# A two-layer hybrid decoder trunk: compression products read the split token pairs, with three smaller moves between engines

## The chip, the cores and the metric

One core of a Trainium2 chip runs the whole program. The metric is device time in microseconds (us), lower is better. TensorE does the matrix products, VectorE and ScalarE the elementwise work, GpSimd some of the same, and all loads go through the queue of SyncE (SP). TensorE's clock has two levels, 1.2 and 2.4 GHz; the profile gives the granted clock as a share of the full one.

## The reference, cut to what matters

512 tokens, width 1024, two layers. Each layer projects the normed rows into the operands of three head groups, joins their outputs by one output projection, and adds a gated feed-forward (2816 wide) and a per-layer embedding. Three pieces matter here:

```python
def compress_blocks(kv, pos_emb, w1, w2):          # 31 blocks of 32 tokens, stride 16
    blocks = kv[:, idx] + pos_emb[:, None, :]
    blocks = blocks.transpose(0, 1, 3, 2, 4).reshape(b, n_cmp, g, NSA_CMP_LEN * d)
    return jax.nn.gelu(blocks @ w1) @ w2
...
    c = jnp.cumsum(log_f.astype(jnp.float32), axis=1).transpose(0, 2, 1)   # forgetting attention
    logits = q @ k * scale + c_blk[..., None] - c[:, :, None, :]
...
    hn = rms_norm(h, norm_ffn[i])
    h = h + (jax.nn.silu(hn @ w_ffn_gate[i]) * (hn @ w_ffn_up[i])) @ w_ffn_down[i]
```

The blocks are made once for keys and once for values, for two groups of heads, each of 64 features.

## The kernel before, in words

Every fp32 matrix product is made of three products of split operands: a high half in the reduced fp32 format that TensorE takes at full rate, a low half with the remainder, high times high, high times low and low times high (`mm3`, L221 to L225). So each operand costs a copy into the high half, on ScalarE, and a subtraction for the low half, on VectorE or GpSimd. Weights come in as raw tiles and are split in `halves` (L197 to L201), where GpSimd takes one subtraction in two or three (`lo_turn`).

A program places each instruction on its engine's queue in an order worked out from the order in the text, priorities (`prio`) and `issue_after`, which only says that one instruction stands behind another on the same engine. Each engine then works through its queue in order.

A layer's attention is a sequence of phases (`spec`, L1175). In each, one attention part is woven with projections as filler: `weave` takes from the stream that is behind by its share, and the numbers after `yield` are the shares in columns of products.

- The compression (`compress`, L563) is woven with the three projections of the stick-breaking heads. The key and value columns come first (`evac_c`, L553): for each of the four tiles of 128 tokens, the rows are rotated, doubled, transposed on TensorE, so that both halves of the partitions hold the same 64 features, and copied by two activations (L561). `blocks` (L567) adds the position embedding to the tokens, even tokens in the upper half of the partitions and odd ones in the lower, in four additions per pass on VectorE (L582), and splits the result into `bhl` by two copies and two subtractions (L589, L590). A pass is made for keys and one for values. `hidden` (L593) then runs 16 pairs of products for each: 128 columns with the high weights (L603), 64 with the low ones (L605), and the GELU chain on VectorE (L611 to L622). Its result is first needed when the selected-block heads begin.
- `forget_rows` (L825) takes the forget gates' logarithms, adds them up along the tokens in one scan on VectorE (L840), and lays the sums out in rows of two tiles that a product can read, with fills of ones and scalings, nearly all on VectorE (L838 to L851). It is called as part "FR" when the second selected-block group starts (L874 is the scores' maximum, L877 their exponential, L869 their products).
- The feed-forward's first unit starts with the first half of the tokens while the second half is still being normed: `part(..., slice(0, 256))` and then `slice(256, 512)` (L1241 to L1246). The norm (`rms_rows`, L328, and `normed`, L345) takes a power on GpSimd for each of the four token tiles (L335), scales the rows on VectorE in two halves (L368), transposes them on TensorE (L380), and splits them on ScalarE (L385) and VectorE (L388). `operand_sums` (L396) prepares sums of operand halves for later units that use seven products instead of eight; for the first half of the tokens it adds on GpSimd, for the second on VectorE (L406).

The small tiles of the GELU chain and the forget rows share four buffers ("e"), the larger ones fifteen ("u").

Of the kernel before, what the change touches and what calls it, by code (L numbers as in the profile page):

```python
# [19 lines left out]
P = 128  # L20
S = 512
# [21 lines left out]
def hybrid_trunk_kernel(  # L43
# [109 lines left out]
    ve.memset(mhalf, -0.5)  # L153

# [241 lines left out]
    def operand_sums(xact):  # L396
# [4 lines left out]
        for kh in range(2):  # L401
            F = utile([P, 2, 4, 256], F32, name="xF")
            for t in range(2):
                hi, lo = (xact.tiles[kh][j][:, :, t * 256:(t + 1) * 256] for j in range(2))
                whole[t, kh] = F[:, t]
                (ve if t else ge).tensor_tensor(F[:, t], f(hi), f(lo), op=ALU.add)  # L406
# [131 lines left out]
    def mixer(i):  # L538
# [10 lines left out]
        ckv = [utile([P, 2, 528], F32, name=f"ckv{j}") for j in range(2)]  # L549
        for t in ckv:  # L550
            ge.memset(t[:, :, S:], 0.0)

        def evac_c(tt, acc):  # L553
# [6 lines left out]
            for j in range(2):  # L560
                se.activation(ckv[j][:, :, tt * P:(tt + 1) * P], pt[:, 2 * j:2 * j + 2, :], AF.Copy)  # L561

        def compress():  # L563
# [3 lines left out]
            def blocks(which, pos, w1, w2):  # L567
# [8 lines left out]
                blk = utile([P, 16, 2, 32], F32, name="blk")  # L576
                tv = ckv[which].rearrange("p g (n l) -> p g n l", l=16)
                for hf in range(2):
                    for par in range(2):
                        r = slice(par * HD, (par + 1) * HD)  # L580
                        src = tv[r, :, hf:hf + 32, par::2].rearrange("p g n l -> p l g n")
                        ve.tensor_tensor(blk[r, 8 * hf:8 * hf + 8], src,  # L582
                                         peT[r, 8 * hf:8 * hf + 8][:, :, None, None].to_broadcast([HD, 8, 2, 32]),
                                         op=ALU.add)
                bhl = utile([P, 2, 16, 64], name="bhl")
                bf = blk.rearrange("p l g n -> p l (g n)")
                for hf in range(2):
                    r = slice(8 * hf, 8 * hf + 8)
                    se.activation(bhl[:, 0, r], bf[:, r], AF.Copy)  # L589
                    ve.tensor_tensor(bhl[:, 1, r], bf[:, r], f(bhl[:, 0, r]), op=ALU.subtract)  # L590
                state.append((w1, w2s, bhl))

            def hidden(which):  # L593
                w1, w2s, bhl = state[which]
# [14 lines left out]
                xx, yy, zz = x1[:, 0:64], x1[:, 64:128], x1[:, 128:192]  # L609
                se.activation(yy, acc[:, 64:128], AF.Copy)  # L610
                ve.tensor_tensor(xx, acc[:, 0:64], yy, op=ALU.add)  # L611
# [8 lines left out]
                gx = x1[:, 256:512].rearrange("p (g h n) -> p g h n", g=2, h=4)  # L620
# [39 lines left out]
            yield 500  # L660
# [164 lines left out]
        def forget_rows():  # L825
# [614 lines left out]
```

## Time and profile before

| | |
|---|---|
| median of 3 runs | 1554.16 us |
| lowest and highest run | 1549.36 and 1555.05 us |
| the profiled execution's own time | 1549.74 us |
| its span, first to last instruction | 1548.0 us |
| TensorE busy | 1490.1 us, 96% |
| VectorE (DVE) busy | 1004.0 us, 65% |
| ScalarE (ACT) busy | 809.3 us, 52% |
| GpSimd (POOL) busy | 650.3 us, 42% |
| granted TensorE clock, mean | 0.990 |

A row of the timeline gives start, length, engine, line, operation, the tiles written and read, their sizes, how many instructions were merged into the row, and in brackets how long the engine had been idle before and what ended that. PEld is the load of weights into TensorE, which overlaps its products. The lengths of successive products overlap; what one costs is read from the distance of their starts. A row of windows gives, for a stretch, the time in which each engine was busy, and the granted clock.

### The profile page before, as it was taken

What the parts mean: (1) busy time and instruction counts of PE and PEld (TensorE: products, weight loads), DVE (VectorE), ACT (ScalarE), POOL (GpSimd) and SP (SyncE); (2) the same over time, 40 slices, a digit from 0 to 9 for tenths busy, and PEclk for the clock granted to TensorE, in tenths of its full rate; (3) what the DMA queues carried; (4) which work ended last, traced back from release to release, by engine and by line L of the source; (5) the groups of instructions that cost most, each with busy time, mean ns of one, the idle gap of its engine ahead of it and who ended that gap; (6) DMA issues with size and microseconds to landing.
All of it is one profiled execution on the core that took longest, in us unless ns stands there. A gap on an engine that the chain in (4) does not pass through costs nothing.

```text
span 1548.0 us, 25774 instructions
## 1 busy us (share of the span) xinstructions
PE 1490.1 (96%) x9562; PEld 1313.8 (85%) x9562; DVE 1004.0 (65%) x1910; ACT 809.3 (52%) x1725; POOL 650.3 (42%) x666
## 2 busy tenths in 40 slices
PE   6999999998999999999999999999899999999998
PEld 5898887878999889988988888778799988998888
DVE  6777869768685257634386878786678833675253
ACT  5466676654544234433355767586545532454243
POOL 3323455554555234431233235465545542455323
PEclk9899999999999999999999999999999999999999
DMA  5421321131333323342224121211223233324321
GB/s 180 118 78 35 84 76 35 49 96 41 105 114 96 95 83 109 123 136 69 83 75 120 55 72 53 82 29 48 90 69 109 89 116 95 107 92 143 109 69 55
DMA packets 114462, 134.75 MB, mean 87 GB/s; under 512 B 6865, under 2 KB 91937, under 8 KB 114337
## 3 DMA queue, kind: packets, MB, share of 16 engines
q1 hardware_dynamic: 114336, 133.10, 28.3%
q8 instruction: 76, 1.25, 0.3%
q14 instruction: 50, 0.40, 0.1%
HBM read 122.59 MB, written 2.10 MB: 81 GB/s over the span
## 4 chain that ended last, share of the span: by engine, by line
PE 78%; DVE 11%; POOL 4%; ACT 3%; issue 2%; DMA 0%; POOLq 0%; ACTq 0%; DVEq 0%
PE acc L222 6%; PE acc L223 6%; PE acc L224 6%; PE st L223 6%; PE st L222 6%; PE st L224 6%; PE gu L223 4%; PE gu L224 4%; PE gu L222 4%; PE accr L222 2%; PE accr L223 2%; PE sc L869 2%; PE accr L224 2%; PE no L1086 2%; PE pTp L890 2%
## 5 line engine op out<-in xcount | busy, mean ns | idle before, releaser
L201 POOL TENSOR_TENSOR whl<-wraw,whl 128x512 fp32r<-128x512 f32 (+2 forms) x196 | 270.0, 1384 | 467.1 <-ACT whl L198 453.7
L198 ACT ACTIVATE whl<-wraw 128x512 fp32r<-128x512 f32 (+2 forms) x312 | 195.1, 631 | 254.4 <-PE acc L224 136.8
L201 DVE TENSOR_TENSOR whl<-wraw,whl 128x512 fp32r<-128x512 f32 x116 | 103.1, 891 | 171.6 <-ACT whl L198 171.3
L449 POOL TENSOR_TENSOR whl<-wraw,whl 128x512 fp32r<-128x512 f32 x78 | 116.1, 1496 | 141.5 <-ACT whl L448 139.2
L223 PE MATMUL acc<-whl,hid 128*128 128x512 f32 x352 | 139.1, 395 | 0.0
L222 PE MATMUL acc<-whl,hid 128*128 128x512 f32 x352 | 139.0, 395 | 0.0
L224 PE MATMUL acc<-whl,hid 128*128 128x512 f32 x352 | 138.8, 394 | 0.0
L223 PE MATMUL gu<-xT,whl 128*128 128x512 f32 (+1 forms) x352 | 124.8, 355 | 0.0
L224 PE MATMUL gu<-xT,whl 128*128 128x512 f32 (+1 forms) x352 | 124.6, 355 | 0.0
L222 PE MATMUL gu<-xT,whl 128*128 128x512 f32 (+1 forms) x352 | 124.0, 354 | 0.0
L449 DVE TENSOR_TENSOR whl<-T,whl 128x512 fp32r<-128x512 f32 x104 | 102.6, 993 | 29.3 <-ACT whl L448 28.9
L223 PE MATMUL st<-X,whl 128*128 128x256 f32 x416 | 116.9, 281 | 0.0
L222 PE MATMUL st<-X,whl 128*128 128x256 f32 x416 | 116.8, 281 | 0.0
L224 PE MATMUL st<-X,whl 128*128 128x256 f32 x416 | 116.6, 280 | 0.0
L882 POOL TENSOR_SCALAR p<-p,rc,gt 128x128 f32<-128x128 f32 (+3 forms) x128 | 79.7, 633 | 71.5 <-DVE rc L880 20.7
L877 ACT ACTIVATE p<-sc,mx 128x128 f32<-128x128 f32 (+3 forms) x160 | 83.9, 535 | 22.4 <-DVE mx L874 20.3
L223 PE MATMUL st<-xT,whl 128*128 128x256 f32 x312 | 87.6, 281 | 0.0
L224 PE MATMUL st<-xT,whl 128*128 128x256 f32 x312 | 87.5, 280 | 0.0
L222 PE MATMUL st<-xT,whl 128*128 128x256 f32 x312 | 87.5, 280 | 0.0
L448 ACT ACTIVATE whl<-T 128x512 fp32r<-128x512 f32 x104 | 64.2, 625 | 42.8 <-PE gu L224 24.2
L896 DVE TENSOR_TENSOR pT<-pTp,pT 128x512 fp32r<-128x512 f32 (+2 forms) x120 | 70.5, 595 | 19.9 <-ACT pT L895 18.9
L895 ACT ACTIVATE pT<-pTp 128x512 fp32r<-128x512 f32 (+2 forms) x120 | 62.2, 528 | 38.2 <-PE pTp L890 36.9
(336 smaller groups left out, 4661.3 us busy)
## 6 DMA issues: line engine op xcount, KB each, us to landing
wraw<-in_w_ffn_gate_dram SPq DMA_DIRECT2D x44, 512.0 KB, 3.6
wraw<-in_w_ffn_up_dram SPq DMA_DIRECT2D x44, 512.0 KB, 4.0
wraw<-in_w_ffn_down_dram SPq DMA_DIRECT2D x44, 512.0 KB, 3.7
wraw<-in_w_in_dram SPq DMA_DIRECT2D x36, 512.0 KB, 3.6
wraw<-in_w_out_dram SPq DMA_DIRECT2D x16, 512.0 KB, 3.6
wraw<-in_w_ple_gate_dram SPq DMA_DIRECT2D x16, 512.0 KB, 3.4
sw<-nq SPq DMA_DIRECT2D x32, 128.0 KB, 2.3
wraw<-in_w_in_dram SPq DMA_DIRECT2D x8, 280.0 KB, 3.0
```

Source lines behind the costliest of these rows:

```text
L198: se.activation(whl[:, 0], raw[:, lo:lo + n], AF.Copy)
L201: eng.tensor_tensor(whl[:, 1], raw[:, lo:lo + n], f(whl[:, 0]), op=ALU.subtract)
L222: i = te.matmul(acc, lhsT=lh, rhs=rh, start=start, stop=False, skip_group_check=True)
L223: te.matmul(acc, lhsT=lh, rhs=rl, start=False, stop=False, skip_group_check=True)
L224: te.matmul(acc, lhsT=ll, rhs=rh, start=False, stop=stop, skip_group_check=True)
L448: se.activation(whl[:, 0], src, AF.Copy)
L449: (ge if n in (1, 2, 3) else ve).tensor_tensor(whl[:, 1], src, f(whl[:, 0]), op=ALU.subtract)
L869: te.matmul(s[:, c:c + w], lhsT=lhsT, rhs=rhs, start=(j == 0), stop=False, skip_group_check=True)
L877: se.activation(e[:, u * n:(u + 1) * n], s[:, u * n:(u + 1) * n], AF.Exp, bias=mx[:, u:u + 1], accum_out=sm[:, u:u + 1])
L882: ge.tensor_scalar(e[:, u * n:(u + 1) * n], e[:, u * n:(u + 1) * n], rc[:, u:u + 1], gates[u] if gates else 1.0, op0=ALU.mult, op1=ALU.mult)
L895: se.activation(hi, src, AF.Copy)
L896: ve.tensor_tensor(lo, src, f(hi), op=ALU.subtract)
```

## The change

The compressed operands are split when the tokens are evacuated: each tile by four activations and four subtractions, even tokens into one half of the partitions, odd tokens into the other, high and low halves side by side. The position embedding is no more added to the tokens: it is written as 16 further positions of the same tile, so that it appears as one more column (two, with a spare) of each product, which now reads every eighth position of the tile. The block tiles, their additions and splits go. After the products, the position's column is added to the others. The forget rows' fills go to GpSimd, the scalings to ScalarE, and the sign to the copy ahead of the scan. The two GpSimd sums of `operand_sums` stand behind the last power of the norm.

```diff
+    one = const.tile([P, 1], F32, name="one")
+    ge.memset(one, 1.0)
...
-                (ve if t else ge).tensor_tensor(F[:, t], f(hi), f(lo), op=ALU.add)
+                with ExitStack() if t else tc.issue_after(latest["pow"].ins):
+                    (ve if t else ge).tensor_tensor(F[:, t], f(hi), f(lo), op=ALU.add)
...
-        ckv = [utile([P, 2, 528], F32, name=f"ckv{j}") for j in range(2)]
+        ckv = [utile([P, 2, 2, 280], name=f"ckv{j}") for j in range(2)]
...
-                se.activation(ckv[j][:, :, tt * P:(tt + 1) * P], pt[:, 2 * j:2 * j + 2, :], AF.Copy)
+                for par in range(2):
+                    r = slice(par * HD, (par + 1) * HD)
+                    hi, lo = (ckv[j][r, t, :, tt * 64:(tt + 1) * 64] for t in range(2))
+                    src = pt[r, 2 * j:2 * j + 2, par::2]
+                    se.activation(hi, src, AF.Copy)
+                    ve.tensor_tensor(lo, src, f(hi), op=ALU.subtract)
...
-                blk = utile([P, 16, 2, 32], F32, name="blk")
-                tv = ckv[which].rearrange("p g (n l) -> p g n l", l=16)
-                for hf in range(2):
-                    for par in range(2):
-                        r = slice(par * HD, (par + 1) * HD)
-                        src = tv[r, :, hf:hf + 32, par::2].rearrange("p g n l -> p l g n")
-                        ve.tensor_tensor(blk[r, 8 * hf:8 * hf + 8], src,
-                                         peT[r, 8 * hf:8 * hf + 8][:, :, None, None].to_broadcast([HD, 8, 2, 32]),
-                                         op=ALU.add)
-                bhl = utile([P, 2, 16, 64], name="bhl")
-                bf = blk.rearrange("p l g n -> p l (g n)")
-                for hf in range(2):
-                    r = slice(8 * hf, 8 * hf + 8)
-                    se.activation(bhl[:, 0, r], bf[:, r], AF.Copy)
-                    ve.tensor_tensor(bhl[:, 1, r], bf[:, r], f(bhl[:, 0, r]), op=ALU.subtract)
-                state.append((w1, w2s, bhl))
+                hi, lo = (ckv[which][:, t, :, 256:272] for t in range(2))
+                src = peT[:, None, :].to_broadcast([P, 2, 16])
+                se.activation(hi, src, AF.Copy)
+                ve.tensor_tensor(lo, src, f(hi), op=ALU.subtract)
+                state.append((w1, w2s))
...
+                pairs = [ckv[which][:, :, :, l:l + 265:8] for l in range(16)]
                 acc = bank("o", name="cmp1")
+                both = acc[:, :136].rearrange("p (t g n) -> p t g n", t=2, g=2)
...
-                            te.matmul(acc[:, :P], lhsT=wv[:, 0, j], rhs=bhl[:, :, l, :], start=(l == 0), stop=False,
+                            te.matmul(both, lhsT=wv[:, 0, j], rhs=pairs[l], start=(l == 0), stop=False,
...
-                            te.matmul(acc[:, :64], lhsT=wv[:, 1, j], rhs=bhl[:, 0, l, :], start=False,
+                            te.matmul(both[:, 0], lhsT=wv[:, 1, j], rhs=pairs[l][:, 0], start=False,
...
-                se.activation(yy, acc[:, 64:128], AF.Copy)
-                ve.tensor_tensor(xx, acc[:, 0:64], yy, op=ALU.add)
+                se.activation(sl, acc[:, 68:136], AF.Copy)
+                ve.tensor_tensor(sb, acc[:, 0:68], sl, op=ALU.add)
+                sb = sb.rearrange("p (g n) -> p g n", g=2)
+                ve.tensor_tensor(xx.rearrange("p (g n) -> p g n", g=2), sb[:, :, :32],
+                                 sb[:, :, 32:33].to_broadcast([P, 2, 32]), op=ALU.add)
...
-                gx = x1[:, 256:512].rearrange("p (g h n) -> p g h n", g=2, h=4)
+                gx = etile("gx1")[:, :256].rearrange("p (g h n) -> p g h n", g=2, h=4)
...
-            blocks(0, pos_k[i], w1_k[i], w2_k[i])
-            yield 5000
-            blocks(1, pos_v[i], w1_v[i], w2_v[i])
-            yield 3000
+            position(0, pos_k[i], w1_k[i], w2_k[i])
+            position(1, pos_v[i], w1_v[i], w2_v[i])
+            yield 7000
             yield from hidden(0)
             yield 2500
             yield from hidden(1)
-            yield 500
+            yield 1500
...
-            se.activation(lft[:4], pt[:4], AF.Copy)
-            ones = etile("ones")
-            ve.memset(ones[:4], 1.0)
+            se.activation(lft[:4], pt[:4], AF.Copy, scale=-1.0)
             cum = etile("cum")
-            ve.tensor_tensor_scan(cum[:4], ones[:4], lft[:4], 0.0, op0=ALU.mult, op1=ALU.add)
+            ve.tensor_tensor_scan(cum[:4], one[:4].to_broadcast([4, S]), lft[:4], 0.0, op0=ALU.mult, op1=ALU.add)
...
             for r in (64, 96):
-                ve.memset(f(fr[r:r + 4]), 1.0)
+                ge.memset(f(fr[r:r + 4]), 1.0)
             for r in (0, 32):
-                ve.memset(f(fl[r:r + 4]), 1.0)
-            ve.tensor_scalar(fr[0:4], cum[:4], -1.0, None, op0=ALU.mult)
-            ve.scalar_tensor_tensor(fr[32:36], cum[:4], -1.0, f(fr[0:4]), op0=ALU.mult, op1=ALU.subtract)
-            ve.tensor_scalar(fl[64:68], f(fr[0:4]), -1.0, None, op0=ALU.mult)
-            ve.tensor_scalar(fl[96:100], f(fr[32:36]), -1.0, None, op0=ALU.mult)
+                ge.memset(f(fl[r:r + 4]), 1.0)
+            se.activation(fr[0:4], cum[:4], AF.Copy)
+            ve.tensor_tensor(fr[32:36], cum[:4], f(fr[0:4]), op=ALU.subtract)
+            se.activation(fl[64:68], cum[:4], AF.Copy, scale=-1.0)
+            se.activation(fl[96:100], f(fr[32:36]), AF.Copy, scale=-1.0)
```

## Rows read from the trace of the kernel before

**Rows 1.** The page's busy shares.

```profile
PE 1490.1 (96%) x9562; PEld 1313.8 (85%) x9562; DVE 1004.0 (65%) x1910; ACT 809.3 (52%) x1725; POOL 650.3 (42%) x666
```

**Rows 2.** TensorE's waits: us in total, times, longest.

```profile
PE xnT L380 <- DVE xn L368: 19.5, 10, 8.0
PE sc L869 <- ACT p L877: 4.7, 2, 2.4
```

**Rows 3.** Windows: stretch, length, PE, PEld, DVE, ACT, POOL busy, PEclk, DMA, GB/s.

```profile
53.52:60.34 6.82, 6.82 (x24) 5.95 (x24) 4.04 (x11) 2.33 (x6) 2.69 (x2) 0.50 0.50 142
...
244.67:248.08 3.41, 3.41 (x11) 2.39 (x11) 2.86 (x14) 2.91 (x11) 2.85 (x6) 0.50 0.00 0
...
1125.31:1128.72 3.41, 3.41 (x18) 3.41 (x17) 3.21 (x5) 0.73 (x2) 0.08 (x1) 0.50 0.00 0
```

**Rows 4.** Timeline of VectorE, 25 to 58 us: the first pass of blocks.

```profile
37.54 5.12 DVE L582 TENSOR_TENSOR blk<-ckv,peT 64x512 f32<-64x512 f32 x4 [0.98 <-ACT peT L575]
42.69 1.36 DVE L590 TENSOR_TENSOR bhl<-blk,bhl 128x512 fp32r<-128x512 f32 x2
```

**Rows 5.** Timeline of ScalarE, 25 to 58 us: the last block copy.

```profile
49.75 0.63 ACT L589 ACTIVATE bhl<-blk 128x512 fp32r<-128x512 f32 x1 [1.50 <-DVE blk L582]
```

**Rows 6.** Timeline of TensorE, 26 to 54 us.

```profile
27.29 0.28 PE L223 MATMUL accr<-whl,xT 128*128 128x256 f32 x1
27.41 0.28 PE L224 MATMUL accr<-whl,xT 128*128 128x256 f32 x1
...
49.80 0.25 PE L605 MATMUL cmp<-bhl,whl 128*128 128x64 f32 x1
49.88 0.30 PE L603 MATMUL cmp<-bhl,whl 128*128 128x128 f32 x1
50.02 0.25 PE L605 MATMUL cmp<-bhl,whl 128*128 128x64 f32 x1
...
51.91 0.33 PE L603 MATMUL cmp<-bhl,whl 128*128 128x128 f32 x1 [0.86 <-ACT whl L198]
53.20 0.30 PE L605 MATMUL cmp<-bhl,whl 128*128 128x64 f32 x1 [0.96 <-DVE whl L201]
```

**Rows 7.** The tile vchl: count, shortest/median/longest in ns, first and last start.

```profile
L644 ACT ACTIVATE vchl<-vcd x2: 259/269/279, 82.7 to 845.0; 128x128 fp32r<-128x128 f32 x2
L645 DVE TENSOR_TENSOR vchl<-vcd,vchl x2: 292/292/292, 83.0 to 845.3; 128x128 fp32r<-128x128 f32 x2
```

**Rows 8.** Timeline of VectorE, 204 to 262 us: forget rows and a maximum.

```profile
235.88 1.11 DVE L847 MEMSET frl<- 4x512 f32 x2
237.03 0.41 DVE L848 TENSOR_SCALAR frl<-cum 4x512 fp32r<-4x512 f32 x1
...
238.19 1.47 DVE L849 SCALAR_TENSOR_TENSOR frl<-cum,frl 4x512 fp32r<-4x512 f32 x1
...
241.17 0.68 DVE L874 TENSOR_REDUCE mx<-sc 128x4 f32<-128x512 f32 x1
```

**Rows 9.** Timelines of TensorE, 204 to 262 and 334 to 385 us: two waits.

```profile
243.96 0.45 PE L869 MATMUL sc<-nk,nq 128*128 128x384 f32 x1 [2.30 <-ACT p L877]
...
362.22 0.63 PE L380 MATMUL xnT<-ident,xn 128*128 128x128 f32 x4 [3.24 <-DVE xn L368]
```

**Rows 10.** Timeline of GpSimd, 353 to 369 us: a sum and the third power.

```profile
358.13 2.36 POOL L406 TENSOR_TENSOR xF<-xT,xT 128x1024 f32<-128x1024 f32 x1
...
360.72 0.57 POOL L335 TENSOR_TENSOR rsr<-rsr,mhalf 128x1 f32<-128x1 f32 x1
```

**Rows 11.** Timelines of GpSimd and VectorE, 778 to 784 us.

```profile
781.10 1.27 POOL L201 TENSOR_TENSOR whl<-wraw,whl 128x512 fp32r<-128x512 f32 x1
...
781.17 1.75 DVE L368 SCALAR_TENSOR_TENSOR xn<-h,rsr,gx 128x512 f32<-128x512 f32 x1 [0.71 <-POOL rsr L335]
```

**Rows 12.** Timeline of VectorE, 334 to 385 us: the fourth tile.

```profile
363.47 1.42 DVE L368 SCALAR_TENSOR_TENSOR xn<-h,rsr,gx 128x512 f32<-128x512 f32 x2 [0.73 <-POOL rsr L335]
...
366.86 1.29 DVE L388 TENSOR_TENSOR xT<-xnT,xT 128x512 fp32r<-128x512 f32 x2 [0.18 <-ACT xT L385]
```

More of the change, by code (lines that the diff above doesn't have):

```diff
@@ L546, in mixer @@
         ge.memset(f(kcv[:, 0:896]), 0.0)
-        ckv = [utile([P, 2, 528], F32, name=f"ckv{j}") for j in range(2)]
+        ckv = [utile([P, 2, 2, 280], name=f"ckv{j}") for j in range(2)]
         for t in ckv:
-            ge.memset(t[:, :, S:], 0.0)
+            ge.memset(f(t[:, :, :, 272:]), 0.0)
         def evac_c(tt, acc):
@@ L560, in evac_c, with position @@
             for j in range(2):
-                se.activation(ckv[j][:, :, tt * P:(tt + 1) * P], pt[:, 2 * j:2 * j + 2, :], AF.Copy)
+                for par in range(2):
[4 more added lines that the diff above has]
+                    ve.tensor_tensor(lo, src, f(hi), op=ALU.subtract)
         def compress():
             state = []
-            def blocks(which, pos, w1, w2):
+            def position(which, pos, w1, w2):
                 pe = etile("pe")[:16, :P]
@@ L575, in blocks @@
                 se.activation(peT, pt[:, 0, :16], AF.Copy)
-                blk = utile([P, 16, 2, 32], F32, name="blk")
-                tv = ckv[which].rearrange("p g (n l) -> p g n l", l=16)
-                for hf in range(2):
-                    for par in range(2):
-                        r = slice(par * HD, (par + 1) * HD)
-                        src = tv[r, :, hf:hf + 32, par::2].rearrange("p g n l -> p l g n")
-                        ve.tensor_tensor(blk[r, 8 * hf:8 * hf + 8], src,
-                                         peT[r, 8 * hf:8 * hf + 8][:, :, None, None].to_broadcast([HD, 8, 2, 32]),
-                                         op=ALU.add)
-                bhl = utile([P, 2, 16, 64], name="bhl")
-                bf = blk.rearrange("p l g n -> p l (g n)")
-                for hf in range(2):
-                    r = slice(8 * hf, 8 * hf + 8)
-                    se.activation(bhl[:, 0, r], bf[:, r], AF.Copy)
-                    ve.tensor_tensor(bhl[:, 1, r], bf[:, r], f(bhl[:, 0, r]), op=ALU.subtract)
-                state.append((w1, w2s, bhl))
+                hi, lo = (ckv[which][:, t, :, 256:272] for t in range(2))
[3 more added lines that the diff above has]
+                state.append((w1, w2s))
             def hidden(which):
-                w1, w2s, bhl = state[which]
+                w1, w2s = state[which]
+                pairs = [ckv[which][:, :, :, l:l + 265:8] for l in range(16)]
                 acc = bank("o", name="cmp1")
+                both = acc[:, :136].rearrange("p (t g n) -> p t g n", t=2, g=2)
                 for u in range(0, 16, 8):
@@ L608, in hidden @@
                 x1 = etile("x1")
-                xx, yy, zz = x1[:, 0:64], x1[:, 64:128], x1[:, 128:192]
-                se.activation(yy, acc[:, 64:128], AF.Copy)
-                ve.tensor_tensor(xx, acc[:, 0:64], yy, op=ALU.add)
+                xx, yy, zz, sl, sb = (x1[:, c:c + n] for c, n in ((0, 64), (64, 64), (128, 64), (192, 68), (260, 68)))
+                se.activation(sl, acc[:, 68:136], AF.Copy)
[3 more added lines that the diff above has]
+                                 sb[:, :, 32:33].to_broadcast([P, 2, 32]), op=ALU.add)
                 ve.tensor_tensor(yy, xx, xx, op=ALU.mult)
```

## The prediction

> **What bounds it now.** The page's busy shares first: TensorE is busy for 1490.1 of 1548.0 us [rows 1]. Some 58 us of idle time, and the stretches at the lower granted clock, are all that a change of other engines' work can win; a product made longer is paid almost in full. So VectorE's 65% and GpSimd's 42% say nothing: an instruction taken off them counts only where TensorE waits behind it. Next, TensorE's waits [rows 2]: the largest group is the norm's transposes behind the scaled rows (19.5 us in ten waits, some of them at the program's start), the next the attention scores (4.7 us in two, one per layer). Then the windows at granted clock 0.50, which is 1.2 instead of 2.4 GHz [rows 3]: 6.82 us in the compression stage (the second layer has a like one from 818.11), 3.41 us behind the scores' wait (again a like one, from 1005.84), and 3.41 us at the second feed-forward's start. Each began behind idle time. All three places are where the change works.
>
> **Compression.** Removed per layer: two passes of four position additions, each pass 5.12 us of VectorE, and two times 1.36 us of splitting [rows 4], 13 us in all, with four copies of about 0.63 us on ScalarE. But TensorE wasn't idle for 13 us: it had the stick-breaking projection to run. What it lost is behind ScalarE: the copies wait in order for VectorE (1.50 us idle ahead of the last) [rows 5], the weight splits stand behind them, and two products start 0.86 and 0.96 us late, at 51.91 and 53.20 [rows 6]; the low clock of rows 3 follows at once. Worth: 2 layers x 1.82 = 3.6 us of idle time, and half of 2 x 6.82 us, 6.8 us, of low clock: **-10.5 us**. Its low end is 0, if the low clock comes for another reason, and the splits are late anyway.
>
> Added: each of the eight token tiles is now evacuated by four activations and four VectorE subtractions on 64 partitions, instead of two activations. No such strided read of PSUM stands in the trace; the nearest are 0.27 us for an activation and 0.29 us for a subtraction of 128 columns [rows 7]. That is 4 x 0.29 = 1.2 us of VectorE per tile, at most 4.7 us a layer if every tile stood on the path; 0 if the projection hides all. Only the last tile, and a transpose bank held longer, can be late, so I take 1 us a layer: **+2.0 us**. If the projection's products weren't there to cover the tiles, it would be the 9.3.
>
> The products themselves: 128 and 64 columns become 136 and 68, now read at every eighth element. One pair takes 0.22 us (49.80 to 50.02), 192 columns; the projection's 256 columns take 0.12 us (27.29 to 27.41) [rows 6], 0.46 ns each. At that rate 192 columns were 0.09 us, so columns don't set the pair's time, and 204 columns could take 1.08 ns each before one is seen. No strided moving operand stands in the trace. Low end: 0. High end: VectorE's strided additions, 5.12 us for 4 x 512 elements [rows 4], 2.5 ns each with their fixed cost: 0.51 us a pair, 64 pairs x 0.29 = +18.6 us. I take 0, since a doubled cost per column would still be hidden. The Trainium skill, SBUF — State Buffer, section "Door 1: The DMA port swizzle", speaks against this: an access that goes to a new 16-byte line each time pays a penalty, and every eighth fp32 is such; it gives no size, and no row here shows it.
>
> The position column, its 64-element correction and two more tiny VectorE steps lie in the GELU chain, whose result the attention needs only much later: 0. The products are emitted slightly earlier and the block tiles' four buffers fall away; the loads on SP's queue keep their order: 0. The new constant is one memset at the start: 0.1 us at most.
>
> **Forget rows.** VectorE loses five fills (two took 1.11 us), three scalings (0.41 us like the first) and keeps the scan and one subtraction (1.47 us before) [rows 8]. Behind the scan stood three of the fills, 1.6 us, and the scalings, 1.25 us, so the first score maximum, at 241.17, moves 2.8 us earlier at least. TensorE went on 2.79 us behind that maximum, at 243.96, and had waited 2.30 us, so from 241.66 [rows 8, 9]. New: 243.96 - 2.8 = 241.16, earlier than it asks. The wait goes in both layers, 4.7 us [rows 2], and with it the low clock, half of 2 x 3.41 [rows 3]: **-8.1 us**. What is late next: three activations of at most 0.63 us each [rows 5] now stand on ScalarE ahead of the score exponentials. Two need only the scan and lie before the maximum; if all three came behind it, 1.9 - 0.5 = 1.4 us of each wait would stay, and its low clock, leaving -1.9. The four fills on GpSimd, at most 0.55 us each, precede a weight split there; TensorE has products in hand, so 0.
>
> **Operand sums.** Two GpSimd sums of about 2.4 us stand ahead of the third tile's power (360.72) [rows 10], and TensorE stood still for 3.24 us until 362.22 [rows 9]; the second layer repeats the wait, and the low clock behind it costs 1.7 us more [rows 3]. Moved behind the fourth tile's power, they let the third tile's rows start about that wait earlier. If that were all: -2 x 3.24 - 1.7 = -8.2 us.
>
> It isn't. At 781.10 a GpSimd split began as a power ended, and the scaling that waited for that power took 1.75 us, until the split had ended, instead of about 0.7 [rows 11]. That is exactly the new order. The fourth tile's two scalings (1.42 us together, from 363.47) then meet the two sums one by one: power at about 360.1, 3.3 earlier, sum to 362.5, first scaling to 363.2, sum to 365.6, second scaling to 366.3, against 364.9 before; its low half, ready at 368.15 before [rows 12], comes between 0.3 us earlier and 1.4 us later, by how VectorE's order falls. The gate's second half of tokens needs it; TensorE runs out of the first half's products before. So the idle time moves from ahead of the third tile to ahead of the fourth. I take **0**; ends -8.2, and +4.5 (2 x 1.4, and 1.7 for a low clock in layer one). The Trainium skill, SBUF — State Buffer, section "Who interferes with whom", has the rule: a VectorE instruction with two inputs in SBUF and a GpSimd instruction that reads SBUF exclude each other for the whole instruction. By that rule, too, the sum is 0 and not -8.2; the trace agrees with it by 1.75 us at 781.17.
>
> **Sum**: -10.5 + 2.0 - 8.1 + 0.0 = -16.6 us, on the profiled execution's own 1549.74 (span 1548.0): 1533.1. That execution was 4.4 us below the median of the runs, 1554.16; on the median the sum gives 1537.6. I say **1537**. A measurement of this kernel tells 0.5%, 7.8 us, from no change: the border is 1546.4.
>
> **Rivals.**
> 1. The forecast: chance 0.50, 1537.
> 2. The exclusion doesn't bite, because the scalings win the port each time or VectorE's order puts other work there: another -8.2, so 1529. For it: the order of arrival decides, and one case [rows 11] is little to go by. Against: that case is the new order itself. Chance 0.18.
> 3. Given back: the strided columns cost half their high end, +9.3 us, or the evacuation stands on the path with its 9.3; 1537 + 9 = 1546. For it: both are unseen, and TensorE has no slack to hide them. Against: the pair's time isn't set by columns. By the skill's rule on 16-byte lines it would be this one, but the rule has no size. Chance 0.20.
> 4. The edit doesn't do what it says for the forget rows: the three activations take VectorE's place as the thing the exponentials wait for, and 6.2 us stay: 1543. Chance 0.07.
> 5. Slower: the strided read itself. It decides from 1.08 ns a column, and eats the whole gain at 0.22 + 16.6/64 = 0.48 us a pair, 2.35 ns a column; half a percent slower needs 24.4/64 = 0.38 us more than now, 2.9 ns a column, over six times the contiguous rate. Then 1562 or more. For it: VectorE's 2.5 ns. Against: those hold fixed costs and a wait. Chance 0.05.
>
> **Numbers.** Faster: all of 1, 2 and 4, less 0.05 for sums of small misses, and 0.08 of rival 3, which straddles the border: 0.78. Same: 0.17. Slower: 0.05. The range goes from all three waits gone with no evacuation cost, 1554.2 - 10.5 - 8.1 - 8.2 = 1527.4, less the 4.4 us between profile and median, 1523, up through rival 3 and the spread of the runs, 1550; rival 5 and a tail stay outside.
>
> **What would show it.** Right: no wait of TensorE for weight splits in the compression stage and granted clock 1.00 where it was 0.50 at 53.52 and 818.11; a pair of compression products still 0.22 us; no wait of the scores behind L877; the third tile's transposes without the 3.24 us, and scalings of the fourth tile stretched to 2 or 3 us beside L406 on GpSimd, with TensorE idle there. Wrong: pairs of 0.3 us or more (3, 5); fourth-tile scalings at 0.7 us (2); score exponentials behind the forget activations (4).

## The result and the profile after

The changed kernel runs in 1539.14 us (median of 6, 1536.30 to 1546.27) beside 1553.82 us before (6 runs): a ratio of 0.992, 95% interval 0.989 to 0.995. A second session of the same kernel, among the experiments, gave 1543.71 us beside 1552.29: 0.993, 0.992 to 0.995. So it is faster by 9 to 15 us. The profiled execution took 1536.46 us (span 1534.5) and is 13.3 us shorter than the profiled one of before; its six runs lie 10 us apart, with mean granted clocks from 0.997 down to 0.992, so what follows goes by stages of one profile.

TensorE is busy for 1482.6 us (97%) of the span after. Three of its waits (us in total, times, longest), which answer to [rows 1, 2]:

```profile
PE xnT L382 <- DVE xn L370: 22.6, 14, 8.0
...
PE sc L871 <- ACT p L879: 1.0, 2, 0.5
...
PE ckvT L563 <- DVE ckv L570: 0.8, 1, 0.8
```

The wait for scores fell from 4.7 to 1.0 us. The largest one, for scaled rows, grew from 19.5 to 22.6 us, in fourteen waits instead of ten: that is where the gain was partly given back.

To see where the time went, the span is cut at the same products of both kernels. Windows of the kernel before (stretch, length, PE, PEld, DVE, ACT, POOL busy, PEclk, DMA, GB/s): layer one up to the first stick-breaking output norm, its forget-row stage, its feed-forward's start; the same of layer two, with the stage between as the fifth row. The feed-forward's start reaches from the transposes of the second tile of tokens to the first product of a unit with seven products:

```profile
0.00:127.00 127.00, 110.73 (x715) 99.75 (x715) 90.86 (x206) 72.18 (x153) 39.78 (x85) 0.96 0.39 114
227.11:295.01 67.90, 64.89 (x380) 51.03 (x380) 58.20 (x143) 48.54 (x125) 36.31 (x53) 0.97 0.13 40
352.94:385.76 32.82, 29.09 (x235) 28.18 (x236) 28.31 (x31) 17.25 (x29) 14.32 (x12) 1.00 0.16 49
772.93:889.00 116.07, 109.80 (x757) 99.21 (x755) 87.93 (x191) 68.58 (x150) 33.88 (x31) 0.97 0.29 84
889.00:989.09 100.09, 97.30 (x694) 85.25 (x694) 75.45 (x201) 68.67 (x167) 48.15 (x54) 1.00 0.26 70
989.09:1056.90 67.81, 64.78 (x380) 51.06 (x379) 58.18 (x143) 48.43 (x125) 36.26 (x53) 0.97 0.14 40
1114.90:1148.56 33.66, 30.38 (x235) 29.66 (x236) 28.32 (x31) 17.22 (x29) 14.29 (x12) 0.95 0.15 48
```

The same seven windows of the kernel after:

```profile
0.00:119.45 119.45, 105.81 (x714) 95.42 (x714) 83.46 (x214) 72.41 (x159) 39.23 (x86) 1.00 0.41 122
219.46:284.58 65.12, 64.41 (x380) 49.74 (x380) 53.01 (x134) 50.52 (x128) 37.68 (x56) 1.00 0.14 41
342.84:377.94 35.10, 30.26 (x235) 29.39 (x236) 33.30 (x32) 17.19 (x29) 13.90 (x12) 0.95 0.15 46
764.89:875.54 110.65, 106.34 (x757) 96.72 (x755) 80.65 (x199) 68.89 (x156) 33.02 (x31) 1.00 0.31 88
875.54:976.82 101.28, 97.68 (x694) 85.44 (x694) 76.55 (x201) 68.71 (x167) 47.53 (x54) 1.00 0.26 69
976.82:1041.90 65.08, 64.40 (x379) 49.73 (x379) 52.91 (x134) 50.52 (x128) 37.65 (x56) 1.00 0.14 41
1100.11:1135.45 35.34, 30.43 (x235) 29.55 (x236) 33.53 (x34) 17.76 (x31) 13.59 (x12) 0.95 0.15 45
```

| stage | layer one | layer two | both | forecast |
|---|---|---|---|---|
| compression (rows 1 and 4) | -7.55 | -5.42 | -13.0 | -8.5 |
| forget rows (rows 2 and 6) | -2.78 | -2.73 | -5.5 | -8.1 |
| operand sums (rows 3 and 7) | +2.28 | +1.68 | +4.0 | 0 |
| layer two between (row 5) | | +1.19 | +1.2 | - |

The rows sum to -13.3 us, against -13.5 us between the starts of the two last products. So the forecast's sum (-16.6) was near because its errors half cancelled. The clock column tells part of it: the compression and forget-row stages run at 1.00 after, and the feed-forward's start at 0.95 in both layers.

What the operand sums did, in the timelines of GpSimd, VectorE and TensorE in layer one of the kernel after:

```profile
351.44 0.57 POOL L337 TENSOR_TENSOR rsr<-rsr,mhalf 128x1 f32<-128x1 f32 x1
351.98 5.11 POOL L409 TENSOR_TENSOR xF<-xT,xT 128x1024 f32<-128x1024 f32 x2
...
352.05 5.58 DVE L370 SCALAR_TENSOR_TENSOR xn<-h,rsr,gx 128x512 f32<-128x512 f32 x2 [0.38 <-POOL rsr L337]
...
348.48 0.63 PE L382 MATMUL xnT<-ident,xn 128*128 128x128 f32 x4 [0.33 <-DVE xn L370]
...
355.02 0.63 PE L382 MATMUL xnT<-ident,xn 128*128 128x128 f32 x4 [2.51 <-DVE xn L370]
357.77 1.09 PE L382 MATMUL xnT<-ident,xn 128*128 128x128 f32 x4 [2.00 <-DVE xn L370]
```

The third tile comes with 0.33 us of wait (3.24 before, [rows 9]), and the fourth tile's two scalings, 1.42 us before [rows 12], take 5.58 us, 2.83 each. They run in turn with the sums: the first sum ends at 354.33, the first scaling at 354.88, the second sum at 357.08, the second scaling at 357.63. TensorE waits 2.51 and 2.00 us for them.

The high-weight product of two successive compression pairs after, and the evacuations of the token tiles (count, shortest/median/longest in ns, first and last start):

```profile
45.23 0.33 PE L605 MATMUL cmp<-ckv,whl 128*128 128x136 f32 x1
...
45.44 0.34 PE L605 MATMUL cmp<-ckv,whl 128*128 128x136 f32 x1
...
L569 ACT ACTIVATE ckv<-ckvT x32: 259/272/275, 30.9 to 795.9; 64x128 fp32r<-64x128 f32 x32
L570 DVE TENSOR_TENSOR ckv<-ckvT,ckv x32: 272/286/296, 32.4 to 796.3; 64x128 fp32r<-64x128 f32 x32
```

A pair, from start to start, still takes 0.21 us, and the evacuations the 0.27 and 0.29 us that [rows 7] gave.

### The profile page after: what moved, and what is told of

The parts are those of the page before. It is cut to its first block, busy times and chain, and to the rows that moved or that the text cites. A ratio compares the mean times of both kernels' runs of the same rounds, so it can differ in the third digit from the quotient of the medians.

```text
span 1534.5 us, 25780 instructions
## 1 busy us (share of the span) xinstructions
PE 1482.6 (97%) x9562; PEld 1305.5 (85%) x9562; DVE 988.7 (64%) x1910; ACT 813.3 (53%) x1743; POOL 649.1 (42%) x675
## 4 chain that ended last, share of the span: by engine, by line
PE 81%; DVE 8%; ACT 4%; POOL 3%; issue 2%; DMA 1%; SPq 0%; POOLq 0%; ACTq 0%; DVEq 0%
PE acc L224 6%; PE acc L225 6%; PE acc L226 6%; PE st L225 6%; PE st L226 6%; PE st L224 6%; PE gu L225 4%; PE gu L226 4%; PE gu L224 4%; PE pTp L892 2%; PE sc L871 2%; PE no L1088 2%; PE accr L224 2%; PE accr L225 2%; PE ge L224 2%; PE accr L226 2%
## 5 line engine op out<-in xcount | busy, mean ns | idle before, releaser
L452 DVE TENSOR_TENSOR whl<-T,whl 128x512 fp32r<-128x512 f32 x104 | 100.3, 971 | 30.1 <-ACT whl L451 29.8
```

Source lines behind the costliest of these rows:

```text
L452: (ge if n in (1, 2, 3) else ve).tensor_tensor(whl[:, 1], src, f(whl[:, 0]), op=ALU.subtract)
```

## The experiments

**Each part alone.** One run takes the moved sums back out of the changed kernel; three put one part each into the kernel before.

```diff
 e1_sums_back: the changed kernel, with
-                with ExitStack() if t else tc.issue_after(latest["pow"].ins):
-                    (ve if t else ge).tensor_tensor(F[:, t], f(hi), f(lo), op=ALU.add)
+                (ve if t else ge).tensor_tensor(F[:, t], f(hi), f(lo), op=ALU.add)
 e2_compression_only, e3_rows_only, e4_sums_only: the kernel before, with
+ evac_c, compress, keys and values as changed / forget_rows and `one` as changed / the two lines above as changed
```

> The changed kernel with only the two GpSimd sums put back where they were before. Theory (from the trace after: the fourth tile's scalings took 2.83 us each beside the sums, and TensorE stood 0.33 + 2.51 + 2.00 us in layer one where it had stood 3.24 + 0.49): the sums' move costs 1.1 us of wait a layer or more, and in layer one half of the 3.41 us of low clock that follows; so this kernel is 3 to 4 us faster than the changed one, with a span of about 1531 against 1534.5, the scalings at 0.7 us and the 3.24 us wait back at the third tile. Rival 1 (the forecast's 0): span within 1 us of 1534.5. Rival 2 (the move pays by its wait at the third tile): 3 us or more slower than the changed kernel.

> The kernel before with only the compression's part of the change. Theory (the distance of the two traces at the first product of the selected-block stage is 7.55 us in layer one, and 5.5 us more are gained by the same place in layer two): -13.0 us, a span of about 1535. Rival (the forecast's terms): -8.5 us, about 1539.5. The distance at the first L780 product of each layer (92.12 and 854.17 before) tells which, free of what the rest of the run does.

> The kernel before with only the forget rows' part. Theory (trace after: from the start of this stage to the end of its scores 2.8 us are gained in layer one and about 1 in layer two, although the wait of 2.3 us and the low clock are both gone, because short gaps between products take the rest): -3.8 us, a span of about 1544. Rival (the forecast's term): -8.1 us, about 1540. Rival 2: the wait was only hidden by something else in the changed kernel, and alone this part gives 0 to -1.

> The kernel before with only the two GpSimd sums moved behind the last power. Theory: the fourth tile's scalings take 2.8 us each instead of 0.7, TensorE's wait goes from the third tile's transposes to the fourth's and grows by about 1.1 us a layer, and the low clock that follows stays; +2 to +4 us, a span of 1550 to 1552. Rival 1 (the forecast's 0): within 1 us of 1548. Rival 2 (the exclusion is of no weight): -8.2 us, about 1540.

| kernel | median, us | ratio to before (95%) | span |
|---|---|---|---|
| sums back (e1) | 1537.77 | 0.992 (0.990 to 0.993) | 1535.6 |
| compression only (e2) | 1541.75 | 0.993 (0.992 to 0.995) | 1537.8 |
| forget rows only (e3) | 1547.61 | 0.997 (0.996 to 0.998) | 1546.2 |
| sums only (e4) | 1557.55 | 1.003 (1.001 to 1.004) | 1556.0 |

The spans were missed by 2 to 5 us. By stages, the compression (13.3 us) and the sums taken back (3.4 us) came as expected, but the forget rows gained more than the 3.8 us expected (5.5), and the sums alone lost more than 2 to 4 (5.5). Windows by the same cuts. Sums back, feed-forward's start of both layers:

```profile
345.26:378.78 33.52, 30.28 (x236) 29.65 (x236) 28.32 (x31) 17.20 (x29) 14.33 (x12) 0.95 0.17 48
1102.93:1136.44 33.51, 30.23 (x235) 29.60 (x236) 28.28 (x31) 17.22 (x29) 14.28 (x12) 0.95 0.17 48
```

Compression only, the first and fourth window, and layer two's forget-row stage:

```profile
0.00:119.17 119.17, 104.78 (x715) 94.41 (x715) 83.53 (x214) 72.50 (x159) 39.44 (x85) 1.00 0.42 122
768.52:879.15 110.63, 106.36 (x756) 96.77 (x754) 80.66 (x199) 68.87 (x156) 33.04 (x31) 1.00 0.32 88
980.40:1047.06 66.66, 63.30 (x379) 49.93 (x379) 58.31 (x143) 48.27 (x125) 36.18 (x53) 1.00 0.14 40
```

Forget rows only, layer one's stage:

```profile
228.20:293.32 65.12, 64.38 (x380) 49.77 (x380) 52.98 (x134) 50.52 (x128) 37.69 (x56) 1.00 0.15 41
```

Sums only, the feed-forward's starts and layer one's scalings:

```profile
354.42:389.90 35.48, 31.16 (x236) 30.20 (x236) 33.67 (x34) 17.76 (x31) 13.63 (x12) 0.90 0.16 45
1120.24:1156.70 36.46, 31.58 (x235) 30.71 (x236) 33.79 (x34) 17.75 (x31) 13.51 (x12) 0.91 0.16 44
...
363.62 5.59 DVE L368 SCALAR_TENSOR_TENSOR xn<-h,rsr,gx 128x512 f32<-128x512 f32 x2 [0.38 <-POOL rsr L335]
```

What follows. Compression alone gains 7.83 and 5.44 us in its two stages: the stage's gain is its own. In layer one, 1.2 us of it come from the program's start, before any work of the compression: the first norm's last transposes began that much earlier in this profile, while they came within 0.1 us of each other in the profiles of before and after. Forget rows alone make the stage 65.12 us, as in the changed kernel; where the low clock happened not to come in the old one (the third compression row, at 1.00) it was 66.66 instead of 67.81 (66.69 in layer two of e4). So of the 2.7 us a layer some 1.1 are the clock and 1.6 the waits. The sums' move is a loss: 2.7 and 2.8 us when put in alone, 1.6 and 1.8 us won back when taken out. The first pair includes low clock (0.90 and 0.91 beside 1.00 and 0.95 before); the second, at 0.95 on both sides, is the move's own price. Of e1's medians that doesn't show (1537.77 beside 1539.14 and 1543.71 in other sessions). By medians, against the 1552.93 us of the kernel before that ran beside them, the three parts make -11.2, -5.3 and +4.6 us, -11.9 together, between the -8.6 and -14.7 of the whole change.

**What stretches the scalings.** If two tensors read from SBUF were the reason, a scaling with one tensor input should run free.

```diff
 e6_one_input: the changed kernel, which leaves out the gain for the fourth tile of the feed-forward's norm
-                        ve.scalar_tensor_tensor(xn, h[:, tt, c], rs, g[:, c], op0=ALU.mult, op1=ALU.mult)
+                        if one_input and tt == NT - 1:
+                            ve.tensor_scalar(xn, h[:, tt, c], rs, None, op0=ALU.mult)
...
```

> The changed kernel, the sums where it put them, but the fourth tile's two scalings of the feed-forward's norm are made with one tensor input (the norm's gain is left out for that tile, so this part of the computation is changed). Theory (it is the second input in SBUF that makes the scaling wait for GpSimd): the two scalings take 0.4 to 0.7 us each although the sums run beside them, and the sums stay at 2.35 us. Rival (any VectorE instruction on SBUF is held by a GpSimd sum, or the sum takes the memory's bandwidth): they take 2 to 3 us each, as the 2.83 us after.

Timelines of GpSimd and VectorE in that kernel, layer one:

```profile
357.30 4.82 POOL L412 TENSOR_TENSOR xF<-xT,xT 128x1024 f32<-128x1024 f32 x2
...
357.37 5.04 DVE L371 TENSOR_SCALAR xn<-h,rsr 128x512 f32<-128x512 f32 x2 [0.38 <-POOL rsr L337]
```

The theory in this form fell: 5.04 us for two, 2.56 each. Three rows of VectorE and one of GpSimd to set beside it. First, of the kernel after, a TENSOR_SCALAR of the same size while GpSimd did nothing; second, of the kernel before, the same one while a weight split ran on GpSimd (255.93 to 257.24); third, of the kernel with the sums back, a sum on GpSimd and the VectorE additions beside it, whose second tensor lies in PSUM:

```profile
294.34 0.48 DVE L962 TENSOR_SCALAR flh<-frl,headsel 128x512 fp32r<-128x512 f32 x1
```

```profile
256.18 1.34 DVE L960 TENSOR_SCALAR flh<-frl,headsel 128x512 fp32r<-128x512 f32 x1
```

```profile
347.65 2.41 POOL L408 TENSOR_TENSOR xF<-xT,xT 128x1024 f32<-128x1024 f32 x1 [3.32 <-DVE xT L390]
...
348.92 1.28 DVE L1108 TENSOR_TENSOR h<-h,acco 128x512 f32<-128x512 f32 x2
```

The additions with one tensor in PSUM took 1.28 us for two beside the sum, no longer than such an addition while GpSimd did nothing (0.68 us at 346.30). So it isn't any VectorE instruction that is held, nor only one with two tensors in SBUF: the one-tensor scaling, at 0.48 us the faster form, is held too. The Trainium skill, SBUF — State Buffer, section "Who interferes with whom", says so: besides two SBUF inputs, `tensor_scalar` is among the forms that can enter a mode with two ports, and then it contends with GpSimd. Here that is 2.56 us beside a sum, and 1.34 us beside a split, instead of 0.48.

**The price of the strided read.** Three times the columns in the compression products, strided for the keys, neighbouring elements for the values (whose compression thus reads other tokens). This run and the one before it were made once each, at 1552.77 and 1544.05 us; only their rows are read.

```diff
 e7_columns: the changed kernel
-                pairs = [ckv[which][:, :, :, l:l + 265:8] for l in range(16)]
+                rows = ckv[which].rearrange("p t g n -> p (t g) n")
+                pairs = [rows[:, :, l:l + 34] if which else rows[:, :, l:l + 265:8] for l in range(16)]
+                high = [t[:, None].to_broadcast([P, 3, 4, 34]) for t in pairs]
+                low = [t[:, None, :2].to_broadcast([P, 3, 2, 34]) for t in pairs]
...
```

> The changed kernel with three times the columns in the compression products (408 and 204, the same operand read three times over): for the keys still at every eighth element, for the values at neighbouring elements (so the values' compression is left wrong). The pair of 136 and 68 strided columns takes 0.21 us and shows no price. Theory A (no price for the stride): pairs of keys and of values take the same time, about 0.28 to 0.30 us (612 columns at the projection's 0.46 ns). Theory B (a price that 204 columns hid, up to the 1.08 ns a column that were free): keys' pairs are longer than the values', up to 0.66 us. Theory C: both are longer than 0.3 us, since repeating costs by itself.

Timeline of TensorE in that kernel: starts of two keys' pairs, then of two values' pairs.

```profile
46.52 0.53 PE L608 MATMUL cmp<-ckv,whl 128*128 128x408 f32 x1
...
47.04 0.54 PE L608 MATMUL cmp<-ckv,whl 128*128 128x408 f32 x1
...
71.22 0.37 PE L608 MATMUL cmp<-ckv,whl 128*128 128x408 f32 x1
...
71.53 0.37 PE L608 MATMUL cmp<-ckv,whl 128*128 128x408 f32 x1
```

A strided pair takes 0.52 us, a contiguous one 0.31: 0.85 against 0.51 ns for each of 612 columns. Theory B holds: a strided column takes 1.7 times as long as a contiguous one. In the changed kernel 204 columns at 0.85 ns are 0.17 us, under the 0.22 us that the pair takes anyway, so nothing of it is seen. The Trainium skill has the rule that an access to a new 16-byte line each time pays a penalty (SBUF — State Buffer, section "Door 1: The DMA port swizzle"). This run agrees with it, with the 1.7 times for every eighth element; no other step was run, so it doesn't show where the penalty begins.

**Other places for the sums.** Five arrangements, and the changed kernel again, in one session with the last three (e9, e11 and e12).

```diff
 e5_sums_held: both GpSimd sums behind a GpSimd instruction that reads the fourth tile's second scaled half
+                if hold and tt == NT - 1 and kh:
+                    latest["hold"] = ge.tensor_scalar(small.tile([P, 1], F32, name="mark"), xn[:, :1], EPS, None, op0=ALU.add)
...
-                with ExitStack() if t else tc.issue_after(latest["pow"].ins):
+                with ExitStack() if t else tc.issue_after(latest["hold"].ins):
 e8_sums_vector: both on VectorE, behind the fourth tile's last subtraction
+                with ExitStack() if t else tc.issue_after(latest["xT"].ins):
+                    ve.tensor_tensor(F[:, t], f(hi), f(lo), op=ALU.add)
 e9_one_early: the first on GpSimd where it was before the change, the second as in e8
 e11_one_held: the first as in e5, the second as in e8
 e12_splits_gpsimd: as e8, and for the first up unit's weights
...
+                    lo_turn[0] = 1 if wi else usual
...
```

> The changed kernel, with one tiny GpSimd instruction (128x1) that reads the fourth tile's second scaled half, and the two GpSimd sums behind it, so that they start when the scalings are done. Theory (the sums and the two-input scalings exclude each other): the scalings take 0.7 us each again, the third tile still comes early (0.33 us of wait, not 3.24), the fourth tile's waits fall from 2.51 + 2.00 us to under 1 together; in each layer the stretch from the third pair of transposes' predecessor (the second tile's) to the first product of the seven-product units is 3 to 4 us shorter than the 35.1 and 35.3 us of the changed kernel, and the low clock may go (1.7 us a layer more); a span of 1524 to 1528, and the best version so far. Rival 1 (what stretched the scalings is not the sums): scalings stay at 2.8 us, 1534.5. Rival 2 (the sums come too late for the units that need them): the scalings are short, but TensorE waits as much ahead of the first seven-product unit, 1533 to 1536.

> The changed kernel with the two first-half sums on VectorE, behind the fourth tile's last subtraction, instead of on GpSimd. Theory: the scalings are 0.7 us again, the waits at the third and fourth tile fall as with the held sums, and VectorE has 2.4 us more ahead of the operand differences, whose first product starts some 15 us later, so most of it is hidden: a span of 1524 to 1530. Rival: VectorE is the chain to the first seven-product unit, and the 2.4 us a layer come back as a wait there: 1530 to 1533.

> The changed kernel itself, unchanged, beside the other arrangements of the sums, so that all have the same chip. Theory (with its runs so far, three at 1536.3 to 1536.7 us and three at 1541.6 to 1546.3 at a lower mean clock): the sums' move costs it 1.4 to 4 us against the kernels with short scalings; a median of 1537 to 1541, and the fourth tile's scalings again 2.83 us each. Rival: on the same chip it is within 1 us of them, and what the traces show there is made up later.

> The changed kernel, with the first of the two sums on GpSimd where it was before the change (ahead of the third tile's power) and the second on VectorE behind the fourth tile's last subtraction. Theory (from the trace of before: one sum of 2.4 us ends about 1 us after the third tile's power could start): TensorE waits 1 to 1.6 us for the third tile instead of 3.24, the scalings take 0.7 us, and the operand differences start as early as after the change; the stretch from the second tile's last transposes to the first seven-product unit takes 31 to 32.5 us, against 35.1 and 35.3 after, 32.9 with the sums held and 33.7 and 32.1 with them on VectorE; a median of 1532 to 1535. Rival: the third tile waits for the whole sum, over 2 us, and the stretch is 33 us or more.

> The changed kernel, with the first sum on GpSimd behind the fourth tile's second scaling (by the same tiny instruction as in the run with held sums) and the second on VectorE behind the fourth tile's last subtraction. With both sums held, GpSimd's weight split came 3 us late behind the second, and TensorE waited 0.54, 1.13 and 0.62 us for splits. Theory: the one sum ends before that split is asked for, VectorE's three sums end about 1 us earlier than with both held, so two of the three waits go, and the stretch takes 31 to 32 us a layer; a median of 1532 to 1534. Rival: the sums of the two engines hold each other up as before, and the stretch stays at 32.9.

> The kernel with both sums on VectorE, and all low-half splits of the first up unit's weights on GpSimd, which was idle there. With the sums on VectorE, TensorE waited 2.05 us for a split that stood behind the operand differences on VectorE. Theory: this wait goes, and the stretch takes 30.5 to 32 us a layer; a median of 1531 to 1534. Rival: GpSimd's splits, stretched to 1.75 and 2.3 us by VectorE's sums, come as late, and the stretch stays at 32 to 33.7.

| kernel | median, us | ratio to before (95%) | stretch, layers one and two, us |
|---|---|---|---|
| changed, again (e10) | 1543.71 | 0.993 (0.992 to 0.995) | 36.00, 35.96 |
| sums held (e5) | 1534.91 | 0.988 (0.986 to 0.990) | 32.87, 32.86 |
| sums on VectorE (e8) | 1536.38 | 0.989 (0.987 to 0.991) | 33.68, 32.10 |
| one early (e9) | 1534.42 | 0.989 (0.987 to 0.990) | 32.40, 32.40 |
| one held (e11) | 1533.60 | 0.988 (0.987 to 0.990) | 32.04, 32.03 |
| sums on VectorE, splits on GpSimd (e12) | 1532.11 | 0.987 (0.986 to 0.988) | 29.81, 29.79 |

The stretches are read as the third and seventh windows above. They hold low clock in e10 (0.91 in both layers, where the first profile of the same kernel had 0.95 and 35.10 and 35.34 us) and in layer one of e8 (0.95), and none in the others. In all but e10 the scalings are 0.7 us again and TensorE waits 0.33 us for the third tile (1.63 in e9). For e5 and e8 the expected spans (1524 to 1528 and 1524 to 1530) were too low, against 1533.1 and 1534.4, and their rivals were half right: the wait went to the weight splits of the up unit. TensorE's waits of e5 from 340 to 380 us, then of e8:

```profile
PE gu L226 <- POOL whl L203: 1.2, 2, 0.6
PE gu L226 <- DVE whl L203: 1.1, 1, 1.1
```

```profile
PE gu L226 <- DVE whl L203: 2.0, 1, 2.0
```

In e5 GpSimd's split stands behind the late sums; in e8 VectorE's split stands behind the differences of the sums. e11 keeps one such wait of 2.0 us. With all of those splits on GpSimd, which the sums had left idle, these waits go. The windows of e12:

```profile
342.27:372.08 29.81, 29.03 (x236) 28.14 (x236) 28.48 (x30) 15.14 (x26) 10.19 (x10) 1.00 0.19 54
1099.86:1129.65 29.79, 28.98 (x235) 28.09 (x236) 28.46 (x30) 15.14 (x26) 10.19 (x10) 1.00 0.19 54
```

TensorE is busy for 29.0 of 29.8 us, at the full clock. e12 is the fastest version: 1532.11 us (1530.98 to 1533.23, 4 runs) beside the 1543.71 of the changed kernel on the same chip, 11.6 us less; the two stretches account for 12.4 (36.00 + 35.96 - 29.81 - 29.79), of which a part is e10's low clock. And 1.3 us a layer come back right behind the stretch: at 372.75 and 375.18 TensorE waits 0.27 and 0.99 us for VectorE, where the changed kernel waits for nothing. The expectation for e10 was missed upwards, by 2.7 us.

## Why the prediction was right or wrong

Faster was right and the time too: 1537 forecast, 1539.14 and 1543.71 measured, within 1523 to 1550. On the profiled executions -13.3 us stand against -16.6. That it came so near is partly luck: the compression gained 4.5 us more than forecast, the other two parts 6.6 us less. By its steps:

- **Compression: the mechanism right, the size too small.** The two splits' waits of 1.8 us a layer are gone, and the low clock with them. Layer two: 5.4 us, where 1.8 + 3.4 - 1.0 was forecast; the 1.0, for the evacuation of tiles, didn't come. Of a tile's transposes one had waited 0.89 us for the rotation before; now one waits 0.77 us for an evacuation (the last of the three waits shown above), and in layer two none does: projection products cover the tiles, as the low bound had it. Layer one: 7.55 us, since a second low-clock stretch of 3.41 us at 74.00, which the prediction's count left out, went as well. Why it came 21 us behind the second wait is open. Of the other two kernels with the old compression, e4 shows a second stretch too (at 76.1), and e3 none, but a first one of 10.24 us instead of 6.83; with the new compression one came in two of eleven profiles (e6 at 78.7, e11 at 77.1).
- **Strided products: 0 taken, 0 measured, and for the reason given.** The estimate of 1.08 ns a column as the point from which it shows stands beside a price of 0.85. Rivals 3 and 5 fell by that, the latter far from its 2.9 ns (rival 3 also by the evacuation, above).
- **Forget rows: -8.1 forecast, -5.5 measured.** The step that failed is "241.16, earlier than it asks". The maximum did come earlier, by 4.25 us counted from the stage's start (241.17 - 227.11 = 14.06 before, 229.27 - 219.46 = 9.81 after), and TensorE went on 2.79 us behind it as before. But it asked earlier too, since the planned order put the scores ahead of more filler: 26 projection products stand between the stage's start and this wait, 38 before. After, in the timelines of VectorE, ScalarE and TensorE:

```profile
229.27 0.68 DVE L876 TENSOR_REDUCE mx<-sc 128x4 f32<-128x512 f32 x1
...
229.99 0.37 ACT L879 ACTIVATE p<-sc,mx 128x128 f32<-128x128 f32 x1 [0.68 <-DVE mx L876]
...
232.06 0.44 PE L871 MATMUL sc<-nk,nq 128*128 128x384 f32 x1 [0.50 <-ACT p L879]
```

  TensorE asked at 231.56, 12.10 us into the stage, before at 14.55; so 0.50 us of wait stay. The clock was priced too high as well: 1.15 us for a stretch of 3.41, not 1.7. Idle time inside it doesn't explain that: TensorE was busy in it throughout in layer one, and for 3.28 us in layer two. With no such stretch, in e2, the stage's busy time was 1.48 us less (63.30 beside 64.78), and its idle time 0.33 us more. Rival 4 fell: ScalarE sat idle for 0.68 us behind the maximum, its three activations were done.
- **Operand sums: 0 taken, +4.0 measured.** The exclusion works as argued from [rows 11], in both layers, sum and scaling in turn. From the end of the fourth tile's power to the end of its second scaling they took 5.62 us (352.01 to 357.63 in the rows of the result above), where the prediction had 6.2 (360.1 to 366.3). The step that failed is "power at about 360.1, 3.3 earlier", on which the bounds "between 0.3 us earlier and 1.4 us later" rest, taken as 0. The fourth tile's power on GpSimd before, and the addition ahead of it after:

```profile
362.86 0.57 POOL L335 TENSOR_TENSOR rsr<-rsr,mhalf 128x1 f32<-128x1 f32 x1
```

```profile
351.18 0.19 POOL L336 TENSOR_TENSOR rsr<-msr,ss 128x1 f32<-128x1 f32 x1 [2.76 <-ACT junk L314]
```

  Counted from the stage's start, it ended at 10.49 us before and at 9.17 after: 1.3 us earlier and not 3.3. GpSimd was free, and waited 2.76 us for the squares of the fourth tile's rows on ScalarE. These came at 8.19 us into the stage, before at 5.77: the third tile's scalings and copies, now early, stood ahead of the fourth tile's last addition on VectorE (6.08 us into the stage, 4.25 before) and ahead of its squares on ScalarE. So the second scaling ended 2.8 us later (14.79 instead of 11.95), beyond the upper bound of 1.4, and the tile's last transposes came 14.93 us into the stage, 13.21 before. In layer two it is 14.96 beside 14.05, since the low clock stood ahead of them there before. Of the +4.0 us some 0.7 are layer one's low-clock stretch (33.52 us with it in e1, 32.82 without it before, both with the old order); with the old order such a stretch came in e1, e2 and e3 too, so it isn't shown to be the move's. Rival 2 fell.
- **Elsewhere, +1.2 us in layer two,** not forecast; it is no part of the change (below).

## What to carry to other kernels

Before a GpSimd instruction is moved, look at what VectorE does beside its new place: with one of two tensors in PSUM it cost nothing here; with both in SBUF, or in a scaling with one, the two took turns, and the wait came back one step later. And ask what else has to be done before an instruction that is to come earlier: here a wait of 3.24 us removed from one tile brought the next one's power 1.3 us forward, because other work had moved ahead of its input. A move off the critical path pays only when the work that it displaces is followed to its next reader; here sums, scalings and weight splits had to be placed together before TensorE stopped waiting. A price that is hidden (here 0.85 instead of 0.51 ns a column) is only hidden up to a size: it is worth measuring at three times that size.

## What the runs showed of the hardware

**A tie between VectorE and GpSimd makes 1.2 us from run to run.** The gated output's scaling (L724, two tensors in SBUF) meets a row of three splits on GpSimd. Timelines of VectorE and GpSimd, first of the kernel after, then of the kernel with the sums back:

```profile
199.93 1.19 DVE L724 SCALAR_TENSOR_TENSOR pair<-pair,hgT,rs 128x512 f32<-128x512 f32 x1
...
200.54 1.75 POOL L203 TENSOR_TENSOR whl<-wraw,whl 128x512 fp32r<-128x512 f32 x1
```

```profile
200.91 2.46 DVE L723 SCALAR_TENSOR_TENSOR pair<-pair,hgT,rs 128x512 f32<-128x512 f32 x1
...
201.50 1.32 POOL L203 TENSOR_TENSOR whl<-wraw,whl 128x512 fp32r<-128x512 f32 x1
```

In the one VectorE gets in between two splits and the next split is longer; in the other it loses to two splits in a row. Over all fourteen profiles the scaling took either 1.2 or 2.5 us, in layer one nine and five times; in layer two it was 1.19 only in the profile of before and 2.5 in all the others, and that is the +1.19 us of the fifth window. Nothing of the change touches it: in layer one the changed kernel itself has 1.19 us in its first profile and 2.45 in its second (e10), and the same stage took 100.01 and 101.26 us.

**The low clock is not the same in each execution of a kernel.** In layer two's compression stage the changed kernel had no such stretch in its first profile (110.65 us) and two of 3.41 us in the second (113.72): some 1.5 us each. The profile of e5 shows none ahead of the program's end, that of sums only six. So a part of 2 us is read from a stage and not from medians of six runs, which for this kernel lay 4.6 us apart in two sessions.
